# A hybrid decoder block on one core: the down projection of its MLP as seven products of halves

## The chip, the core and the metric

The kernel runs on one core of a Trainium2 chip. The core's engines work side by side, each through its own list of instructions in order: TensorE (PE, matrix products into PSUM), VectorE (DVE), ScalarE (ACT), GpSimd (POOL) and SyncE (SP), which issues the transfers from memory. They wait for each other by semaphores. The metric is the device time of one execution in microseconds (us).

## The reference

One layer on 512 tokens of width 1024, in float32: token mixing (attention heads and a short convolution), then the gated MLP. The part that matters here is its end.

```python
h = rms_norm(x, norm_ffn_pre[l])                        # (512, 1024)
gu = causal_dwconv(h @ w_ffn_up[l], ffn_conv_w[l])      # (512, 5632), a convolution of three taps
g, up = jnp.split(gu, 2, axis=-1)
y = (jax.nn.gelu(g, approximate=True) * up) @ w_ffn_down[l]   # (512, 2816) @ (2816, 1024)
x = x + rms_norm(y, norm_ffn_post[l])
```

## The kernel before

A float32 product runs as three passes over operands that are split exactly into a high and a low part: high x high, low x high, high x low. A split is two operations, one of ACT that rounds (`split`, L131, or `Stream._split`, L84) and one of DVE that subtracts (L132, L85). So each product of a 128x128 and a 128x512 tile is three matmuls.

The dense weights come through `Stream`: tiles of 128x1024 in the order of their use, loaded by SP into three raw buffers, split into a ring of four buffers, two tiles ahead of PE. Before the down projection, the up projection (L829 to L844) makes 44 tiles of 128 channels x 512 tokens. Per tile PE runs 24 matmuls from the transposed activations h2T (L166 to L169), ACT and DVE do the convolution (L825 to L827), and for each of the 22 pairs of gate and value ACT applies the gelu (L842), DVE multiplies (L843), and the product is split into aT (L844).

The down projection (L846 to L877) sums over the 22 tiles f of 128 channels. Each tile of weights (128 channels x 1024 columns) meets the activations of four token tiles t and two column halves hf: 8 x 3 = 24 matmuls a tile (`one`, L739), into all eight banks of PSUM, one for each (t, hf). After 19 tiles, the last three are taken token tile by token tile (`token_major`, L730), so that a finished one can be normed and stored while PE works on the next: ACT squares and sums (L865), DVE multiplies by the gains (L866), POOL takes the reciprocal root (`rstd_of`, L248), DVE multiplies and adds the residual (L873), SP stores. POOL has no other work in this stage.

The order on each engine is set by a scheduler when the program is built, mostly that of the code, with later instructions moved ahead where buffers are free.

Of the kernel before, what the change touches and what calls it, by code (L numbers as in the profile page):

```python
# [54 lines left out]
class Stream:  # L55
    """The dense weights in the order of their use: loaded some tiles ahead, split fewer ahead."""

    def __init__(self, tc, nc, raw, ring, items, loads=3, splits=2):
# [49 lines left out]
def block_kernel(ctx: ExitStack, tc: tile.TileContext, a, out):  # L108
# [52 lines left out]
    items += [(a["w_d"][f * P:(f + 1) * P, :], 1024, f"d{f}") for f in range(NF)]  # L161
# [31 lines left out]
    # the tensor engine's clock comes up while the first loads are under way  # L193
# [6 lines left out]
    # bias tables: U[p, h, u] = -(bias of distance p + 384 - u), +BIG where it is negative  # L200
    # row r of vrows is the whole of vd; reading with a pitch one short shifts it by r
# [544 lines left out]
    with tc.tile_pool(name="ph2", bufs=1, reuse_waits="tile") as ph2:  # L746
# [49 lines left out]
        # the first tiles of the MLP in halves of the tokens, behind the norm of the last rows  # L796
# [20 lines left out]
    ph3 = ctx.enter_context(tc.tile_pool(name="ph3", bufs=1, reuse_waits="tile"))  # L817
    aT = ph3.tile([P, NF, 2, S], F32R, name="aT")
# [12 lines left out]
    for n, m in enumerate(UP):  # L831
# [7 lines left out]
        if m >= NF:  # L839
# [13 lines left out]
    for f in range(NF - LAST):
        w = W.next()
        for th in banks:
            one(ys[th], dacts, w, f, *th, f == 0, False)
# [81 lines left out]
```

## Time and profile before

| what | us |
|---|---|
| median of the runs (634.5, 637.78, 637.83) | 637.78 |
| span of the profiled execution | 633.9 |
| up projection, PE | 272.0 to 507.6 |
| down projection, PE | 507.6 to 627.1 |
| its end, after the last matmul's start | 627.1 to 633.9 |

The profile is of one execution, whose own time is not given beside its span; by the runs it lies 0.6 to 3.9 us above it. A duration of a matmul overlaps its neighbours', so PE's pace is read from starts. In "idle before" the time stands that an engine waited, and what ended it.

### The profile page before, as it was taken

The page shows a single profiled execution, that of the slowest core. Times are in us where ns is not written, and L with a number is a line of the kernel's source. Part 1 is how long each engine was busy: PE and PEld are TensorE (multiplying, and loading weights), DVE is VectorE, ACT ScalarE, POOL GpSimd, SP SyncE. Part 2 cuts the span into 40 slices and gives each one's busy share as a digit, 9 for nine tenths or more (in the row PEclk, how much of TensorE's full clock was granted, in tenths as well). Part 3 has the DMA queues.
Part 4 walks back from the last instruction along what each step waited for, and adds up shares of the span by engine and source line. Part 5 has one row for each costly group of instructions (what it writes and reads, how often), then busy time and mean ns, then how long its engine had stood idle before and what let it go on. Part 6 is the DMA issues. An engine that isn't in the chain of part 4 may idle for free.

```text
span 633.9 us, 8027 instructions
## 1 busy us (share of the span) xinstructions
PE 617.5 (97%) x2980; PEld 511.3 (81%) x2980; DVE 382.2 (60%) x668; ACT 306.5 (48%) x556; POOL 62.7 (10%) x88
## 2 busy tenths in 40 slices
PE   8998899999999999999999999999999999999995
PEld 6886688887778788898888888888888888888884
DVE  5379967898988756648666656565656542222225
ACT  6546765798878644426443434444344422222212
POOL 1102453002130202200000000000000000000001
PEclk9999899999999999999999999999999999999999
DMA  8993355201121483004222233232322232232203
GB/s 293 329 304 129 133 180 189 74 10 43 42 78 53 169 280 130 8 5 143 93 96 98 99 100 101 100 100 99 101 87 95 89 114 87 94 100 99 67 0 133
DMA packets 25302, 72.00 MB, mean 114 GB/s; under 512 B 3136, under 2 KB 7048, under 8 KB 25008
## 3 DMA queue, kind: packets, MB, share of 16 engines
q1 hardware_dynamic: 25264, 71.50, 33.9%
q8 instruction: 23, 0.38, 0.2%
q14 instruction: 15, 0.12, 0.1%
HBM read 67.50 MB, written 4.74 MB: 114 GB/s over the span
## 4 chain that ended last, share of the span: by engine, by line
PE 80%; DVE 10%; DMA 3%; ACT 3%; issue 2%; POOL 1%; SPq 0%; DVEq 0%; POOLq 0%; ACTq 0%
PE pu L168 13%; PE pu L169 13%; PE pu L167 13%; PE z L743 6%; PE z L742 6%; PE z L744 6%; PE y L744 2%; PE y L743 2%; PE y L742 2%; DVE x L417 2%; DMA raw_q<-in_w_t 2%; PE tr L622 2%; PE sc L593 2%; PE o L631 1%; PE o L630 1%
## 5 line engine op out<-in xcount | busy, mean ns | idle before, releaser
L167 PE MATMUL pu<-h2T,w_u 128*128 128x512 f32 (+1 forms) x384 | 142.8, 372 | 0.0
L168 PE MATMUL pu<-h2T,w_u 128*128 128x512 f32 (+1 forms) x384 | 142.7, 372 | 0.0
L169 PE MATMUL pu<-h2T,w_u 128*128 128x512 f32 (+1 forms) x384 | 142.6, 371 | 0.0
L167 PEld LDWEIGHTS pu<-h2T,w_u 128*128 128x128 f32 x384 | 72.3, 188 | 12.6
L168 PEld LDWEIGHTS pu<-h2T,w_u 128*128 128x128 f32 x384 | 72.3, 188 | 12.6 <-DVE h2T L132 0.2
L169 PEld LDWEIGHTS pu<-h2T,w_u 128*128 128x128 f32 x384 | 72.3, 188 | 12.4
L826 DVE SCALAR_TENSOR_TENSOR cv<-pu,ffnw,cv 128x511 f32<-128x511 f32 x44 | 32.9, 749 | 70.2 <-ACT cv L825 70.2
L85 DVE TENSOR_TENSOR w_d<-raw_d,w_d 128x1024 fp32r<-128x1024 f32 x22 | 26.9, 1224 | 72.8 <-ACT w_d L84 72.8
L742 PE MATMUL z<-w_d,aT 128*128 128x512 f32 x176 | 68.5, 389 | 0.0
L743 PE MATMUL z<-w_d,aT 128*128 128x512 f32 x176 | 68.5, 389 | 0.0
L744 PE MATMUL z<-w_d,aT 128*128 128x512 f32 x176 | 68.5, 389 | 0.0
L825 ACT ACTIVATE cv<-pu,ffnw 128x512 f32<-128x512 f32 x44 | 30.3, 688 | 64.0 <-PE pu L169 63.9
L84 ACT ACTIVATE w_d<-raw_d 128x1024 fp32r<-128x1024 f32 x22 | 23.3, 1059 | 75.2 <-PE z L744 75.2
L85 DVE TENSOR_TENSOR w_u<-raw_u,w_u 128x1024 fp32r<-128x1024 f32 x44 | 53.4, 1217 | 5.9 <-ACT w_u L84 5.8
L84 ACT ACTIVATE w_u<-raw_u 128x1024 fp32r<-128x1024 f32 x44 | 46.2, 1052 | 6.6 <-PE pu L169 6.3
L599 ACT ACTIVATE P<-P,mins 128x512 f32<-128x512 f32 (+3 forms) x64 | 35.4, 554 | 11.5 <-DVE mins L597 11.1
L742 PEld LDWEIGHTS z<-w_d,aT 128*128 128x128 f32 x176 | 33.0, 188 | 6.9
L744 PEld LDWEIGHTS z<-w_d,aT 128*128 128x128 f32 x176 | 33.0, 188 | 6.9
L743 PEld LDWEIGHTS z<-w_d,aT 128*128 128x128 f32 x176 | 33.0, 188 | 6.7
L131 ACT ACTIVATE aT<-cv 128x512 fp32r<-128x512 f32 x22 | 13.9, 632 | 49.5 <-DVE cv L843 49.5
L251 POOL TENSOR_SCALAR rsz<-ssz 128x1 f32<-128x1 f32 x4 | 1.2, 300 | 355.2 <-ACT jz L865 355.2
L827 DVE SCALAR_TENSOR_TENSOR cv<-pu,ffnw,cv 128x510 f32<-128x510 f32 x44 | 32.8, 748 | 1.5
(215 smaller groups left out, 1158.7 us busy)
## 6 DMA issues: line engine op xcount, KB each, us to landing
raw_u<-in_w_u SPq DMA_DIRECT2D x44, 512.0 KB, 3.3
raw_d<-in_w_d SPq DMA_DIRECT2D x22, 512.0 KB, 3.2
raw_c<-in_w_c SPq DMA_DIRECT2D x8, 512.0 KB, 3.3
raw_o<-in_w_o SPq DMA_DIRECT2D x8, 512.0 KB, 3.4
vrows<-vd SPq DMA_DIRECT2D x2, 1280.0 KB, 10.4
xT<-in_xT SPq DMA_DIRECT2D x8, 256.0 KB, 5.3
xt<-in_x SPq DMA_DIRECT2D x4, 512.0 KB, 7.1
raw_q<-in_w_t SPq DMA_DIRECT2D x4, 512.0 KB, 7.0
```

Of the source, the lines that this page charges most:

```text
L84: self.nc.scalar.activation(t[:, 0, cs], self.raws[n][:, cs], AF.Copy)
L85: eng.tensor_tensor(t[:, 1, cs], self.raws[n][:, cs], f32(t[:, 0, cs]), op=ALU.subtract)
L167: MM(dst, wh, xh, start=first, stop=False)
L168: MM(dst, wh, xl, start=False, stop=False)
L169: MM(dst, wl, xh, start=False, stop=last)
L599: act(v, v, AF.Exp, bias=m, scale=-1.0, accum_out=self.sums[:, r, b:b + 1])
L742: MM(y, oh_, w[:, 0, cs], start=first, stop=False)
L743: MM(y, ol_, w[:, 0, cs], start=False, stop=False)
L744: MM(y, oh_, w[:, 1, cs], start=False, stop=last)
L825: act(t, pu, AF.Copy, scale=ffnw[:, m, 2:3])
L826: nc.vector.scalar_tensor_tensor(t[:, 1:], pu[:, :S - 1], ffnw[:, m, 1:2], t[:, 1:], op0=ALU.mult, op1=ALU.add)
L827: nc.vector.scalar_tensor_tensor(t[:, 2:], pu[:, :S - 2], ffnw[:, m, 0:1], t[:, 2:], op0=ALU.mult, op1=ALU.add)
```

## The change

The down product is cut in halves in three ways: tokens (0 to 255 and 256 to 511), channels (even and odd tiles f) and columns (0 to 511 and 512 to 1023). With A11, A12, A21, A22 the four parts of the activations (rows are tokens, columns are even and odd channels) and B11, B12, B21, B22 those of the weights, seven products take the place of eight:

- phase a: A11 x B11 into banks zx, (A21 + A22) x T1 into zy, with T1 = B12 - B11
- phase b: (A11 - A21) x (B22 - B12) into zw, S2 x T2 on top of zx, with S2 = A21 + A22 - A11 and T2 = B22 - T1
- phase c: A12 x B21 into zz, A22 x (B21 - T2) on top of zw
- phase d: (A12 - S2) x B22 on top of zy

Each phase runs over the 11 pairs j of channel tiles, d in six steps of two pairs and one. A product is 2 token tiles x 3 matmuls a pair, so a tile of a, b or c has 12 matmuls and each is still 128x128 by 128x512. The sums and differences of the weights are POOL's (L859, L865, L866, L872, L923), in the raw tile and in a tile `tres` that takes the buffer of h2T; those of the activations are POOL's too (L907, L911, L912 in the up stage, L939 later). What they give is split as before, now in pieces of 128x512 (`part`, L103, L104, and `split`, L149, L150). Between the phases the banks are copied (L985, L988, L1014) or added up (L1011, L1015); the two second products of b and c add onto banks that were filled before, and so begin after these reads. In phase d and behind it, what remains is added (L998) ahead of the square and the gains. The weights of the down projection are loaded by halves, those of B12, B21 and B22 apart; B22 and B12 twice.

```diff
+        if isinstance(src, list):
+            for at, part in src:
+                self.nc.sync.dma_start(t[:, at:at + 512], part)
...
+    def part(self, t, cs, src):
+        self.nc.scalar.activation(t[:, 0, cs], src, AF.Copy)
+        self.nc.vector.tensor_tensor(t[:, 1, cs], src, f32(t[:, 0, cs]), op=ALU.subtract)
...
-    items += [(a["w_d"][f * P:(f + 1) * P, :], 1024, f"d{f}") for f in range(NF)]
+    wd = lambda f, n: a["w_d"][f * P:(f + 1) * P, n * 512:(n + 1) * 512]
+    items += [(a["w_d"][2 * j * P:(2 * j + 1) * P, :], 1024, f"da{j}") for j in range(NJ)]
+    items += [([(0, wd(2 * j + 1, 1)), (512, wd(2 * j, 1))], 1024, f"db{j}") for j in range(NJ)]
+    items += [([(0, wd(2 * j + 1, 0))], 1024, f"dc{j}") for j in range(NJ)]
+    items += [([(512 * n, wd(2 * j + 1, 1)) for n, j in enumerate(js)], 512 * len(js), f"dd{js[0]}") for js in DJ]
...
+    def made_b(j):
+        def f(raw, t):
+            nc.gpsimd.tensor_tensor(raw[:, hi_], raw[:, lo_], raw[:, hi_], op=ALU.subtract)
+            nc.gpsimd.tensor_tensor(tres[j], raw[:, lo_], tres[j], op=ALU.subtract)
+            return (lo_, raw[:, hi_]), (hi_, tres[j])
+        return f
...
-            nc.vector.tensor_tensor(tg, tg, tu, op=ALU.mult)
-            split(aT[:, f, 0, :], aT[:, f, 1, :], tg)
+            if f % 2 == 0:
+                nc.vector.tensor_tensor(tg, tg, tu, op=ALU.mult)
+                even = tg.rearrange("p (m c) -> p m c", m=2)
+                nc.gpsimd.tensor_tensor(sb[:, jj, 0], even[:, 0], even[:, 1], op=ALU.subtract)
+            else:
+                odd = sc_[:, jj]
+                nc.vector.tensor_tensor(odd.rearrange("p m c -> p (m c)"), tg, tu, op=ALU.mult)
+                nc.gpsimd.tensor_tensor(even[:, 1], even[:, 1], odd[:, 1], op=ALU.add)
+                nc.gpsimd.tensor_tensor(sb[:, jj, 1], even[:, 1], even[:, 0], op=ALU.subtract)
+                t = ah["a", jj] = acts_tile(f"aa{jj}")
+                split(t[:, 0], t[:, 1], even)
...
+    whole = hpool.tile([P, 16, 512], F32, tag="hT", name="tres")
...
+            split(t[:, 0], t[:, 1], src[:, j])
+            if ph == "b":
+                nc.gpsimd.tensor_tensor(sb[:, j, 1], sc_[:, j, 0], sb[:, j, 1], op=ALU.subtract)
...
+    phase("a", (bx, by), (True, True), 2)
+    c1, c57, c2 = [], [], []
+    for m in range(2):
+        c1.append(spare[m])
+        act(c1[m], bx[m], AF.Copy)
...
+    phase("b", (bw, bx), (True, False), 1)
...
+    for m in range(2):
+        nc.vector.tensor_tensor(c57[m], bw[m], c57[m], op=ALU.add)
...
+    phase("c", (bz, bw), (True, False), 1)
...
+    for m in range(2):
+        for n in range(tail, len(DJ)):
+            for i in range(len(DJ[n])):
+                prod(by, m, tiles[n], ah["d", n], i, False, n == len(DJ) - 1 and i == len(DJ[n]) - 1)
+        half_done(m, 1, by[m], c2[m])
+        tile_done(m)
```

Where the emitted order differs. On POOL, before, the norm of the last rows of the mixing part (rs) is followed at once by the first of the MLP's four (rsz):

```order
L252 TENSOR_TENSOR rsy3_2754<-rsy3_2754,mhalf_122 128x1
L251 TENSOR_SCALAR rs2_3_2762<-ss2_3_2757 128x1
L252 TENSOR_TENSOR rs2_3_2762<-rs2_3_2762,mhalf_122 128x1
L251 TENSOR_SCALAR rsz0_5067<-ssz0_5049 128x1
L252 TENSOR_TENSOR rsz0_5067<-rsz0_5067,mhalf_122 128x1
```

On POOL, after, this stands at the edge of phases a and b (raw_da and raw_db are loaded weights, tres the differences, sb and sc activations, of 256 tokens each half):

```order
L859 TENSOR_TENSOR tres_4499<-raw_da10_4626 128x512
L866 TENSOR_TENSOR tres_4499<-raw_db0_4646,tres_4499 128x512
L865 TENSOR_TENSOR raw_db0_4646<-raw_db0_4646 128x512
L939 TENSOR_TENSOR sb_3010<-sc_3011,sb_3010 128x256
L866 TENSOR_TENSOR tres_4499<-raw_db1_4667,tres_4499 128x512
L865 TENSOR_TENSOR raw_db1_4667<-raw_db1_4667 128x512
L939 TENSOR_TENSOR sb_3010<-sc_3011,sb_3010 128x256
```

Between rs2_3 and the first rsz there were no rows, and there are now 88 operations: 33 of 128x256 on the activations of the up stage, and 44 of 128x512 on the weights with 11 of 128x256 among them, the first four of these ahead of the up stage's last two.

On DVE, before, the down stage has one split a tile of weights and nothing else:

```order
L85 TENSOR_TENSOR w_d15_4865<-raw_d15_4781,w_d15_4865 128x1024
L85 TENSOR_TENSOR w_d16_4894<-raw_d16_4810,w_d16_4894 128x1024
L85 TENSOR_TENSOR w_d17_4923<-raw_d17_4839,w_d17_4923 128x1024
L85 TENSOR_TENSOR w_d18_4952<-raw_d18_4868,w_d18_4952 128x1024
L85 TENSOR_TENSOR w_d19_4981<-raw_d19_4897,w_d19_4981 128x1024
```

On DVE, after, at the edge of b and c (w_db and w_dc are split weights, ac the split activations of phase c, zw a bank of PSUM):

```order
L104 TENSOR_TENSOR w_db10_4961<-raw_db10_4892,w_db10_4961 128x512
L104 TENSOR_TENSOR w_db10_4961<-tres_4499,w_db10_4961 128x512
L150 TENSOR_TENSOR ac6_5176<-sc_3011,ac6_5176 128x512
L104 TENSOR_TENSOR w_dc0_4986<-raw_dc0_4918,w_dc0_4986 128x512
L104 TENSOR_TENSOR w_dc0_4986<-tres_4499,w_dc0_4986 128x512
L150 TENSOR_TENSOR ac7_5200<-sc_3011,ac7_5200 128x512
L104 TENSOR_TENSOR w_dc1_5010<-raw_dc1_4943,w_dc1_5010 128x512
L104 TENSOR_TENSOR w_dc1_5010<-tres_4499,w_dc1_5010 128x512
L150 TENSOR_TENSOR ac8_5224<-sc_3011,ac8_5224 128x512
L104 TENSOR_TENSOR w_dc2_5041<-raw_dc2_4968,w_dc2_5041 128x512
L104 TENSOR_TENSOR w_dc2_5041<-tres_4499,w_dc2_5041 128x512
L1011 TENSOR_TENSOR tres_4499<-zw0_4510,tres_4499 128x512
```

A tile now takes three operations of half the size in place of one, and the read of zw stands nine operations behind the last split of phase b.

On DVE, before, the last two token halves end the program like this (z a bank, tz its normed rows):

```order
L866 TENSOR_TENSOR tz30_5153<-z30_4486,gpo_5035 128x512
L866 TENSOR_TENSOR tz31_5166<-z31_4487,gpo_5035 128x512
L873 SCALAR_TENSOR_TENSOR tz30_5153<-tz30_5153,rsz3_5169,x1_2408 128x512
L873 SCALAR_TENSOR_TENSOR tz31_5166<-tz31_5166,rsz3_5169,x1_2408 128x512
```

On DVE, after, the last rows are of token tiles 0 and 1 (zy a bank, c2 a copy of another):

```order
L998 TENSOR_TENSOR tz01_5425<-zy0_4508,c20_5035 128x512
L1000 TENSOR_TENSOR tz10_5390<-tz10_5390,gpo_4514 128x512
L1000 TENSOR_TENSOR tz01_5425<-tz01_5425,gpo_4514 128x512
L1007 SCALAR_TENSOR_TENSOR tz00_5384<-tz00_5384,rsz0_5430,x1_2408 128x512
L1007 SCALAR_TENSOR_TENSOR tz01_5425<-tz01_5425,rsz0_5430,x1_2408 128x512
L998 TENSOR_TENSOR tz11_5446<-zy1_4509,c21_5038 128x512
L1000 TENSOR_TENSOR tz11_5446<-tz11_5446,gpo_4514 128x512
L1007 SCALAR_TENSOR_TENSOR tz10_5390<-tz10_5390,rsz1_5451,x1_2408 128x512
L1007 SCALAR_TENSOR_TENSOR tz11_5446<-tz11_5446,rsz1_5451,x1_2408 128x512
```

An addition has come ahead of ACT's square, and the last one stands behind both products of the tile before.

## Rows read from the trace of the kernel before

**Rows 1.** The page's head and its busy times by engine.
```profile
span 633.9 us, 8027 instructions
...
PE 617.5 (97%) x2980; PEld 511.3 (81%) x2980; DVE 382.2 (60%) x668; ACT 306.5 (48%) x556; POOL 62.7 (10%) x88
```

**Rows 2.** Two stretches, up and down projection; columns in the first line.
```profile
core 0: us, PE busy (x) PEld busy (x) DVE busy (x) ACT busy (x) POOL busy (x), PEclk, DMA share, GB/s
272.00:507.60 235.60, 235.60 (x1113) 198.19 (x1112) 142.51 (x175) 100.35 (x134) 0.00 (x0) 1.00 0.29 95
507.60:627.10 119.50, 119.50 (x529) 98.91 (x527) 34.63 (x36) 26.18 (x35) 2.58 (x6) 1.00 0.24 83
```

**Rows 3.** In order of time, PE (start us, duration us, instruction).
```profile
507.63 0.39 PE L742 MATMUL z<-w_d,aT 128*128 128x512 f32 x1
...
508.31 0.39 PE L742 MATMUL z<-w_d,aT 128*128 128x512 f32 x1
```

**Rows 4.** Groups by line, down stage (xcount, busy us, mean ns, idle before).
```profile
L742 PE MATMUL z<-w_d,aT 128*128 128x512 f32 x176 | 68.5, 389 | 0.0
...
L85 DVE TENSOR_TENSOR w_d<-raw_d,w_d 128x1024 fp32r<-128x1024 f32 x19 | 23.3, 1225 | 72.8 <-ACT w_d L84 72.8
```

**Rows 5.** In order of time, POOL, then DVE, near 182 us.
```profile
182.59 1.09 POOL L505 TENSOR_TENSOR cz<-cz,Rb 128x512 f32<-128x512 f32 x1 [2.60 <-DVE sums L604]
...
182.62 1.09 DVE L606 TENSOR_TENSOR sums<-sums,G 128x2 f32<-128x2 f32 x1
```

**Rows 6.** In order of time, POOL, then DVE, 100 to 107 us.
```profile
100.30 1.09 POOL L505 TENSOR_TENSOR cz<-cz,Rb 128x512 f32<-128x512 f32 x1 [4.63 <-DVE cz L504]
...
105.16 2.19 POOL L511 TENSOR_TENSOR ct<-ct,Rb 128x512 f32<-128x512 f32 x1 [2.12 <-DVE ct L509]
...
100.62 1.85 DVE L85 TENSOR_TENSOR w_tx<-raw_tx,w_tx 128x1024 fp32r<-128x1024 f32 x1 [0.40 <-ACT w_tx L84]
...
105.00 1.21 DVE L85 TENSOR_TENSOR w_tb<-raw_tb,w_tb 128x1024 fp32r<-128x1024 f32 x1
```

**Rows 7.** In order of time, POOL, then DVE, near 187 us.
```profile
187.47 1.29 POOL L511 TENSOR_TENSOR ct<-ct,Rb 128x512 f32<-128x512 f32 x1 [2.07 <-DVE ct L509]
...
187.64 0.69 DVE L132 TENSOR_TENSOR ptl<-tr,pth 128x512 fp32r<-128x512 f32 x1
```

**Rows 8.** In order of time, POOL near 81 us.
```profile
81.10 2.41 POOL L85 TENSOR_TENSOR w_c<-raw_c,w_c 128x1024 fp32r<-128x1024 f32 x1 [2.60 <-ACT w_c L84]
```

**Rows 9.** In order of time, DVE, two operations back to back.
```profile
72.71 0.68 DVE L132 TENSOR_TENSOR ptl<-tr,pth 128x512 fp32r<-128x512 f32 x1
73.31 0.68 DVE L372 TENSOR_TENSOR qt<-pp_q,Rb 128x512 f32<-128x512 f32 x1
```

**Rows 10.** The page's DMA issues, loads of the down weights.
```profile
raw_d<-in_w_d SPq DMA_DIRECT2D x22, 512.0 KB, 3.2
```

**Rows 11.** In order of time, all engines, the kernel's end.
```profile
627.08 0.39 PE L744 MATMUL z<-w_d,aT 128*128 128x512 f32 x1
627.57 0.60 ACT L865 ACTIVATE jz<-z 128x512 f32<-128x512 f32 x1 [1.33 <-PE z L744]
...
628.35 0.30 POOL L251 TENSOR_SCALAR rsz<-ssz 128x1 f32<-128x1 f32 x1 [3.14 <-ACT jz L865]
628.73 0.56 POOL L252 TENSOR_TENSOR rsz<-rsz,mhalf 128x1 f32<-128x1 f32 x1
629.33 1.41 DVE L873 SCALAR_TENSOR_TENSOR tz<-tz,rsz,x 128x512 f32<-128x512 f32 x2 [0.35 <-POOL rsz L252]
```

**Rows 12.** In order of time, PE; then a stretch (columns: rows 2).
```profile
64.25 0.40 PE L167 MATMUL pp_q<-hT,w_q 128*128 128x512 f32 x1
67.60 0.45 PE L622 MATMUL tr<-ident,P 128*128 128x128 f32 x1 [2.96 <-ACT P L613]
67.71 0.77 PE L168 MATMUL pp_q<-hT,w_q 128*128 128x512 f32 x1
...
68.00:70.00 2.00, 2.00 (x7) 1.51 (x6) 1.92 (x4) 1.84 (x4) 0.00 (x0) 0.50 0.04 14
```

More of the change, by code (lines that the diff above doesn't have):

```diff
@@ L39 @@
 NF = DFF // P
+NJ = NF // 2
+DJ = [list(range(j, min(j + 2, NJ))) for j in range(0, NJ, 2)]
 EPS = 1e-6
@@ L66, in __init__ @@
         self.other = {}
+        self.made = {}
+        self.cap = 10000
     def _load(self):
@@ L79, in _split @@
         t = pool.tile([P, 2, 1024], F32R, tag=tag, bufs=bufs, name=f"w_{name}")
+        if name in self.made:
+            for cs, src in self.made[name](self.raws[n], t):
+                self.part(t, cs, src)
+            self.tiles.append(t)
+            return
         eng = self.nc.gpsimd if name in self.pool_lo else self.nc.vector
@@ L817, in block_kernel, with acts_tile, made_a, f @@
     ph3 = ctx.enter_context(tc.tile_pool(name="ph3", bufs=1, reuse_waits="tile"))
-    aT = ph3.tile([P, NF, 2, S], F32R, name="aT")
+    sb = ph3.tile([P, NJ, 2, 256], F32, name="sb")
+    sc_ = ph3.tile([P, NJ, 2, 256], F32, name="sc")
+    def acts_tile(name):
+        return ph3.tile([P, 2, 2, 256], F32R, tag="ah", bufs=NJ, name=name)
+    ah = {}
+    lo_, hi_ = slice(0, 512), slice(512, 1024)
+    tres, late_t1 = [], []
+    def made_a(j):
+        def f(raw, t):
+            if not tres:
+                late_t1.append((j, raw, t))
+                return [(lo_, raw[:, lo_])]
+            nc.gpsimd.tensor_tensor(tres[j], raw[:, hi_], raw[:, lo_], op=ALU.subtract)
+            return (lo_, raw[:, lo_]), (hi_, tres[j])
+        return f
+    def made_b(j):
+        def f(raw, t):
+            nc.gpsimd.tensor_tensor(raw[:, hi_], raw[:, lo_], raw[:, hi_], op=ALU.subtract)
+            nc.gpsimd.tensor_tensor(tres[j], raw[:, lo_], tres[j], op=ALU.subtract)
+            return (lo_, raw[:, hi_]), (hi_, tres[j])
+        return f
+    def made_c(j):
+        def f(raw, t):
+            nc.gpsimd.tensor_tensor(tres[j], raw[:, lo_], tres[j], op=ALU.subtract)
+            return (lo_, raw[:, lo_]), (hi_, tres[j])
+        return f
+    for j in range(NJ):
+        W.made[f"da{j}"], W.made[f"db{j}"], W.made[f"dc{j}"] = made_a(j), made_b(j), made_c(j)
+    W.cap = next(n for n, x in enumerate(W.items) if x[2] == "da0") + 3
     def cv(name):
@@ L853, in block_kernel @@
[L853 to L856, printed above, removed]
+            jj = f // 2
+            if f % 2 == 0:
+                nc.vector.tensor_tensor(tg, tg, tu, op=ALU.mult)
+                even = tg.rearrange("p (m c) -> p m c", m=2)
+                nc.gpsimd.tensor_tensor(sb[:, jj, 0], even[:, 0], even[:, 1], op=ALU.subtract)
+            else:
+                odd = sc_[:, jj]
[4 more added lines that the diff above has]
+                split(t[:, 0], t[:, 1], even)
@@ new lines, in block_kernel, with acts_ready @@
+    W.cap = 10000
+    whole = hpool.tile([P, 16, 512], F32, tag="hT", name="tres")
+    tres += [whole[:, j] for j in range(NJ)]
+    spare = [whole[:, 12 + n] for n in range(4)]
+    for j, raw, t in late_t1:
+        nc.gpsimd.tensor_tensor(tres[j], raw[:, hi_], raw[:, lo_], op=ALU.subtract)
+        W.part(t, hi_, tres[j])
+    def acts_ready(ph, j):
+        if ph == "a" or (ph, j) in ah:
+            return
+        t = ah[ph, j] = acts_tile(f"a{ph}{j}")
+        if ph == "d":
+            js = DJ[j]
+            n = slice(0, len(js))
+            split(t[:, 0, n], t[:, 1, n], sb[:, js[0]:js[-1] + 1, 1])
+        else:
+            src = sb if ph == "b" else sc_
+            split(t[:, 0], t[:, 1], src[:, j])
+            if ph == "b":
+                nc.gpsimd.tensor_tensor(sb[:, j, 1], sc_[:, j, 0], sb[:, j, 1], op=ALU.subtract)
@@ new lines, in block_kernel, with prod @@
+    bx = [pt_bank(f"zx{m}") for m in range(2)]
+    by = [sc_bank(f"zy{m}") for m in range(2)]
+    bw = [mm_bank(f"zw{m}") for m in range(2)]
+    bz = [mm_bank("zz0"), o_bank("zz1")]
+    def prod(bk, m, t, x, n, first, last):
+        cs = slice(n * 512, (n + 1) * 512)
+        tok = slice(m * P, (m + 1) * P)
+        MM(bk[m], x[:, 0, n, tok], t[:, 0, cs], start=first, stop=False, skip_group_check=True)
+        MM(bk[m], x[:, 1, n, tok], t[:, 0, cs], start=False, stop=False, skip_group_check=True)
+        MM(bk[m], x[:, 0, n, tok], t[:, 1, cs], start=False, stop=last, skip_group_check=True)
@@ new lines, in phase, with second @@
+    def phase(ph, banks, opens, skew):
+        tiles = []
+        def second(j):
+            for m in range(2):
+                prod(banks[1], m, tiles[j], ah[ph, j], 1, opens[1] and j == 0, j == NJ - 1)
+        for j in range(NJ):
+            w = W.next()
+            acts_ready(ph, j)
+            tiles.append(w)
+            for m in range(2):
+                prod(banks[0], m, w, ah[ph, j], 0, opens[0] and j == 0, j == NJ - 1)
+            if j == skew:
+                for i in range(skew):
+                    second(i)
+            if j >= skew:
+                second(j)
+            nxt = {"a": "b", "b": "c", "c": "d"}[ph]
+            if j + 1 < NJ:
+                acts_ready(ph, j + 1)
+            elif ph != "c":
+                acts_ready(nxt, 0)
@@ L857, in block_kernel, with half_done @@
     gpo = ph3.tile([P, D], F32, name="gpo")
     nc.sync.dma_start(gpo, a["g_ffn_post"].broadcast_to([P, D]))
+    phase("a", (bx, by), (True, True), 2)
[3 more added lines that the diff above has]
+        act(c1[m], bx[m], AF.Copy)
+    for m in range(2):
+        c57.append(spare[2 + m])
+        act(c57[m], by[m], AF.Copy)
+    phase("b", (bw, bx), (True, False), 1)
     fin = {}
-    def half_done(t, hf):
-        if hf == 0:
+    def half_done(t, hf, y, other):
+        if t not in fin:
@@ L874, in tile_done @@
             nc.sync.dma_start(out[t * P:(t + 1) * P, cs], fin[t, hf])
-    wl = [W.next(1) for _ in range(LAST)]
-    token_major(wl, ys, dacts, half_done, tile_done, list(range(NF - LAST, NF)))
+    for m in range(2):
+        nc.vector.tensor_tensor(c57[m], bw[m], c57[m], op=ALU.add)
+    for m in range(2):
+        c2.append(cv(f"c2{m}"))
+        act(c2[m], bx[m], AF.Copy)
+        nc.vector.tensor_tensor(c57[m], bx[m], c57[m], op=ALU.add)
+    phase("c", (bz, bw), (True, False), 1)
+    tail = len(DJ) - 2
+    tiles = []
+    for n, js in enumerate(DJ):
+        w = W.next(2)
+        tiles.append(w)
+        acts_ready("d", n)
+        if n + 1 < len(DJ):
+            acts_ready("d", n + 1)
+        if n < tail:
+            for m in range(2):
+                for i in range(len(js)):
+                    prod(by, m, w, ah["d", n], i, False, False)
+        if n == 0:
+            for m in range(2):
+                t = 2 + m
+                fin[t] = stat(f"ssz{t}")
+                half_done(t, 0, bw[m], c2[m])
+        if n == 1:
+            for m in range(2):
+                t = 2 + m
+                tt, junk = cv(f"tz{t}1"), cv(f"jz{t}1")
+                act(junk, c57[m], AF.Square, scale=1.0 / 32.0, accum_out=fin[t][:, 1:2])
+                nc.vector.tensor_tensor(tt, c57[m], gpo[:, 512:], op=ALU.mult)
+                fin[t, 1] = tt
+                tile_done(t)
+        if n == 2:
+            for m in range(2):
+                half_done(m, 0, bz[m], c1[m])
+    for m in range(2):
+        for n in range(tail, len(DJ)):
[3 more added lines that the diff above has]
+        tile_done(m)
 def _bucket_onehot():
```

18 lines of the change are left out of this document (7 added, 11 removed).

## The prediction

> **What bounds the kernel now.** I read the page's head and the table of stretches first. TensorE (PE) is busy for 97% of the 633.9 us, VectorE (DVE) for 60%, GpSimd (POOL) for 10% [rows 1]. In the down projection, 507.6 to 627.1, PE is busy for all of 119.50 us at the full clock, DVE for 34.63 and POOL for 2.58 [rows 2]: the stage is bound by its matmuls alone. Its pace is read from starts, since the durations overlap: one operand triple begins at 507.63 and the next at 508.31 [rows 3], so a matmul costs 0.68 / 3 = 0.2267 us, and 528 of them 119.7 us, which is the stage. One DVE split of 1.22 us per 24 matmuls (5.44 us) lies under them [rows 4]. The span ends 6.6 us after the last matmul's slot (627.08 + 0.23).
>
> Against its own time: the profiled execution's span is 633.9 us; the runs shown are 634.5 to 637.83 with median 637.78, so 0.6 to 3.9 us lie around a span. I work out the change of the span and add it to the median.
>
> **What goes.** Seven products of halves need 7/8 of the matmuls: 66 fewer of 528, 66 x 0.2267 = **-15.0 us**. The 33 tiles of phases a, b and c have 12 matmuls each, 2.72 us a tile and 29.9 us a phase; phase d has 66, 15.0 us.
>
> **What comes: a shared resource.** Each tile now has combinations on POOL and twice the splits on DVE: per tile of a one POOL subtraction of 128x512, of b two (the weights) and mostly one of 128x256, of c one; on DVE two splits of weights and one of activations, 128x512 each. Taken alone each engine fits, or nearly: 2 x 1.29 + 0.72 = 3.3 us of POOL and 3 x 0.60 of DVE in b. The question is whether they run at the same time. The rows say no. At 182.59 POOL reads two tiles for 1.09 us, and a DVE operation on 128x2, begun 0.03 us later, lasts 1.09 us too [rows 5]. At 100.30 POOL works until 101.39; DVE's split, begun at 100.62, lasts 1.85 us instead of 1.22 and ends 1.08 us after POOL. At 105.00 DVE begins first and ends at 106.21; POOL, begun at 105.16, lasts 2.19 and ends 1.14 us after DVE [rows 6]. While one of them runs, the other stands, and then needs most of its own time. A DVE operation with one operand in PSUM (tr) ran in its ordinary 0.69 us beside POOL [rows 7], so only DVE operations with two SBUF operands count: all the splits of the down stage.
>
> [...]
>
> Prices in the queue: POOL 128x512 alone 1.29 [rows 7], after a DVE operation 1.14 [rows 6]. 128x1024 takes 2.41 [rows 8], so 512 elements more cost 1.13; 128x256 is then about 0.72 alone (estimate), 0.58 in the queue. DVE 128x512 in the queue: half of 1.08, 0.54, say 0.55; back to back 0.60 (72.71 to 73.31) [rows 9].
>
> **The walk.** PE begins phase a at 507.6 as before. The tile for the differences takes h2T's place, so POOL cannot begin before the last up matmul: three subtractions from 507.9. The load of da3 needs the raw buffer of da0, free after the second of them (507.9 + 2 x 1.29 = 510.5), and lands 3.2 us later [rows 10], at 513.7. From there the queue is full. Until the last POOL operation of phase b, the two orders hold 30 POOL operations of 512, 13 of 256 and 54 DVE splits: 30 x 1.14 + 13 x 0.58 + 54 x 0.55 = 34.2 + 7.5 + 29.7 = 71.4 us, to 585.1. PE, unhindered, would have finished b at 507.6 + 59.8 = 567.4. This is the main cost: **about 18 us late at that point**.
>
> Then the edge of b and c. The second product of c adds onto the banks zw, which DVE must first read (L1011), and in DVE's order that read stands behind the splits of dc0 to dc2. From 585.1: three POOL subtractions, each with a DVE split (1.69), then POOL waits for a load and eight DVE splits run at 0.60: 5.1 + 4.8 = 9.9, to 595.0; the read 0.7, so PE goes on at 595.7. By then it has done 12 of c's 132 matmuls; 120 x 0.2267 = 27.2 brings it to 622.9. POOL and DVE have less than that left in c (8 x 1.14, 23.5 x 0.55 and four reads at 0.60: 24.5), so PE bounds c from there. Phase d has no POOL work, its 1.22 us splits lie under 2.72 us of matmuls: 15.0, to 637.9.
>
> The like edge of a and b (the copy L985 stands on ScalarE behind the splits of db2) leaves PE idle for about 5 us at 549 to 554, but b waits for the queue anyway, and PE's 2.72 us a tile against the queue's 4.0 to 4.5 makes it up. Cost 0; without that cover about 5.
>
> The end. Before, from the last slot (627.31): ScalarE at 627.57, POOL's root, DVE's two last products to 630.74 (629.33 + 1.41), then 3.2 to the span's end [rows 11]. After, the last half is first added to c2 on DVE (0.73), and that add (tz11) stands behind tile 0's two products. Tile 0's last matmul lies 9 x 0.2267 = 2.04 before the end; its add (0.26 + 0.73) and the 3.17 us from ScalarE's start to the products' end make 4.16, so tz11 begins 2.12 after the last slot, and its own chain ends 2.12 + 0.73 + 3.17 = 6.02 after it, against 3.43 before: **+2.6 us**.
>
> Sum: 637.9 + 6.6 + 2.6 = 647.1 against 633.9: **+13.2 us**. On the median: **651 us**.
>
> Edits priced at nothing. In the up stage, three POOL operations of 256 per four up tiles (21.8 us): DVE there is busy for 142.51 of 235.60 us [rows 2], which hides 2.2 us of blocking per 21.8; uncovered it would be 11 x 2.2 = 24 us, which I exclude since PE there is fed two splits ahead. The loads grow from 11 to 17 MB; the DMA engines are busy for 24% [rows 2]. The matmuls' shape is the same.
>
> Bounds of the queue: with POOL at the quickest two-input row (1.09, 0.95 in the queue) 30 x 0.19 = 5.7 us less; with every operation at its full price alone (1.29, 0.72, DVE 0.60), 80.5 instead of 71.4, 9.1 us more. I take the middle value because rows 6 show this very alternation. Span +7.5 to +22.
>
> **Rivals.**
> 1. *They run side by side after all* (the stalls of rows 5 and 6 were waits for something else). Then b is bound by POOL at 22 x 1.29 + 6 x 0.72 = 32.7 against 29.9, and the change is -15.0 + 2.8 + 2.6 + 1 at the start = -8.6: 629 us. Against it: an operation on two columns stretched to POOL's 1.09 us.
> 2. *The queue is shorter, and comes out even.* POOL at 0.95 and 0.46, and the edge at L1011 gone since POOL's last three subtractions are already done when DVE comes to ac6 (-5): 71.4 - 5.7 - 1.6 - 5 gives about +1: 639 us. For it: the 1.09 of rows 5 and 6; against it: the 1.09 reads from column 2 on (L505), the operations here from aligned columns, as L511 with its 1.29 [rows 7].
> [...]
> 4. *It computes something else, or not seven products*: the emitted order of PE has 66 matmuls fewer, so no.
>
> **How the numbers follow.** Slower by the queue, 642 to 660: 0.73. Rival 3: 0.10. Rival 2: 0.09. Rival 1: 0.08. About 0.5% (3.2 us) is what a measurement of this kernel tells from no change, so "same" is 634.6 to 641. Faster 0.08; same 0.10 (rival 2 and the low edge of the forecast); slower 0.82. The range for 8 in 10 is 640 to 661: it leaves out rival 1, most of rivals 2 and 3.
>
> **What would show it.** PE in the down stage: 462 matmuls and about 20 us idle, most of it in phase b, where PE waits for DVE's splits. DVE's 128x512 splits there have a mean well over 0.69 us (near 1.2 to 1.7), POOL's subtractions over 1.29 (near 1.7). A row of POOL and a row of DVE overlap in time, but the later one ends about one own duration after the earlier. The last slot lies near 638, and 9 us follow it. Wrong it would be if DVE's splits keep 0.69 beside a working POOL (rival 1), if PE's idle time in b is under 5 us (rival 2), or if the granted clock is near 0.5 through b (rival 3).

## The result, and the profile after

The changed kernel takes 655.97 us (median of 4 runs, 654.34 to 656.36) where the one before takes 636.14 (633.9 to 637.83): a ratio of 1.0322, with a 95% interval of 1.0286 to 1.0358. The forecast was 651, counted on the median of 637.78 known then (a ratio of 1.021), with a range of 640 to 661, slower. The span of the profiled execution is 652.6 us, 18.7 more than before; the forecast was +13.2.

The table of stretches of the kernel after, one row for each of the phases a, b, c and d (columns as in [rows 2]):

```profile
506.40:542.30 35.90, 32.16 (x133) 24.08 (x132) 34.27 (x30) 17.77 (x31) 30.19 (x22) 1.00 0.47 159
542.30:589.40 47.10, 36.80 (x133) 25.39 (x132) 47.10 (x35) 22.17 (x42) 41.81 (x28) 0.93 0.33 108
589.40:627.40 38.00, 32.99 (x133) 26.40 (x132) 34.08 (x40) 18.66 (x31) 14.05 (x9) 0.91 0.39 124
627.40:642.40 15.00, 15.00 (x67) 12.21 (x65) 12.64 (x19) 7.27 (x17) 4.57 (x5) 1.00 0.26 91
```

Before, one row answered to these four: 119.50 us with PE busy in all of it [rows 2]. Now a, b and c take 35.9, 47.1 and 38.0 where 12 x 11 matmuls need 29.9 each, and only d, without weight differences, runs at PE's pace. In b the busy engines are DVE (all 47.10) and POOL (41.81), and yet their 35 and 28 operations would take some 24 and 32 us at the durations of undisturbed ones (0.68 on DVE, as at 585.34; on POOL 1.29 to 1.30 for 128x512, as in [rows 7] and at 506.64, and 0.74 for 128x256, as at 303.9). The groups of b show the same by their means (128x512 each; xcount | busy us, mean ns):

```profile
L865 POOL TENSOR_TENSOR raw_db<-raw_db 128x512 f32<-128x512 f32 x11 | 19.0, 1728 | 0.0
L866 POOL TENSOR_TENSOR tres<-raw_db,tres 128x512 f32<-128x512 f32 x11 | 18.5, 1684 | 2.2 <-DMA raw_db<-in_w_d 2.2
L104 DVE TENSOR_TENSOR w_db<-tres,w_db 128x512 fp32r<-128x512 f32 x11 | 18.4, 1671 | 0.0
...
L104 DVE TENSOR_TENSOR w_db<-raw_db,w_db 128x512 fp32r<-128x512 f32 x11 | 17.2, 1565 | 0.0
```

How that comes about is seen in single rows of b, POOL first, then DVE, in order of time (start, duration):

```profile
557.03 1.74 POOL L865 TENSOR_TENSOR raw_db<-raw_db 128x512 f32<-128x512 f32 x1
558.73 1.19 POOL L939 TENSOR_TENSOR sb<-sc,sb 128x256 f32<-128x256 f32 x1
559.88 1.74 POOL L866 TENSOR_TENSOR tres<-raw_db,tres 128x512 f32<-128x512 f32 x1
561.59 1.73 POOL L865 TENSOR_TENSOR raw_db<-raw_db 128x512 f32<-128x512 f32 x1
```

```profile
557.54 1.77 DVE L104 TENSOR_TENSOR w_db<-tres,w_db 128x512 fp32r<-128x512 f32 x1
559.24 1.23 DVE L150 TENSOR_TENSOR ab<-sb,ab 128x512 fp32r<-128x512 f32 x1
560.39 1.78 DVE L104 TENSOR_TENSOR w_db<-raw_db,w_db 128x512 fp32r<-128x512 f32 x1
562.09 1.77 DVE L104 TENSOR_TENSOR w_db<-tres,w_db 128x512 fp32r<-128x512 f32 x1
```

Read the ends: POOL's row of 557.03 ends at 558.77, DVE's of 557.54 at 559.31, 0.54 later; POOL's next ends at 559.92, 0.61 after that. Both engines are "busy" without a gap, but at each moment one of them works and the other's row is running while it waits. The period of a pair is 559.24 - 557.54 = 1.70 us, for 1.14 + 0.55 = 1.69 forecast; with a 128x256 it is 1.15, for 1.13.

The edge of b and c, PE's row with its wait and DVE's read:

```profile
592.49 0.51 PE L952 MATMUL zz<-w_dc,ac 128*128 128x512 f32 x1 [1.05 <-DVE w_dc L104]
597.65 0.79 PE L950 MATMUL zw<-w_dc,ac 128*128 128x512 f32 x1 [3.96 <-DVE tres L1011]
598.25 0.63 PE L951 MATMUL zw<-w_dc,ac 128*128 128x512 f32 x1
598.67 0.63 PE L952 MATMUL zw<-w_dc,ac 128*128 128x512 f32 x1
...
602.92 0.40 PE L950 MATMUL zz<-w_dc,ac 128*128 128x512 f32 x1
```

```profile
595.25 1.75 DVE L104 TENSOR_TENSOR w_dc<-tres,w_dc 128x512 fp32r<-128x512 f32 x1
596.92 1.28 DVE L1011 TENSOR_TENSOR tres<-zw,tres 128x512 f32<-128x512 f32 x2
```

PE stands for 4 us until the read is done. The twelve matmuls behind it start 0.60, then 0.41 to 0.43 us apart in place of 0.2267, and the granted clock in 598.0 to 602.6 is 0.50.

The end, rows of PE, DVE, ACT, POOL in order of time (they answer to [rows 11]):

```profile
642.14 0.39 PE L952 MATMUL zy<-w_dd,ad 128*128 128x512 f32 x1
...
643.61 1.41 DVE L1007 SCALAR_TENSOR_TENSOR tz<-tz,rsz,x 128x512 f32<-128x512 f32 x2 [0.84 <-POOL rsz L277]
...
644.94 0.68 DVE L998 TENSOR_TENSOR tz<-zy,c 128x512 f32<-128x512 f32 x1
645.71 0.63 ACT L999 ACTIVATE jz<-tz 128x512 f32<-128x512 f32 x1 [3.68 <-DVE tz L998]
...
646.47 0.69 DVE L1000 TENSOR_TENSOR tz<-tz,gpo 128x512 f32<-128x512 f32 x1 [0.85 <-ACT jz L999]
646.53 0.79 POOL L276 TENSOR_SCALAR rsz<-ssz 128x1 f32<-128x1 f32 x1 [2.96 <-ACT jz L999]
647.41 0.56 POOL L277 TENSOR_TENSOR rsz<-rsz,mhalf 128x1 f32<-128x1 f32 x1
648.00 1.41 DVE L1007 SCALAR_TENSOR_TENSOR tz<-tz,rsz,x 128x512 f32<-128x512 f32 x2 [0.84 <-POOL rsz L277]
```

From the last matmul's start to the span's end it is now 652.6 - 642.14 = 10.5 us; before, 633.9 - 627.08 = 6.8.

### The profile page after: what moved, and what is told of

The parts are those of the page before. It is cut to its first block, busy times and chain, and to the rows that moved or that the text cites. A ratio compares the mean times of both kernels' runs of the same rounds, so it can differ in the third digit from the quotient of the medians.

```text
span 652.6 us, 8230 instructions
## 1 busy us (share of the span) xinstructions
PE 613.5 (94%) x2914; PEld 499.3 (77%) x2914; DVE 467.8 (72%) x745; ACT 336.9 (52%) x629; POOL 176.4 (27%) x176
## 4 chain that ended last, share of the span: by engine, by line
PE 69%; DVE 22%; issue 3%; ACT 3%; POOL 2%; DMA 1%; SPq 0%; DVEq 0%; POOLq 0%; ACTq 0%
PE pu L193 12%; PE pu L192 12%; PE pu L194 12%; DVE w_db L104 5%; PE y L768 2%; PE y L769 2%; PE y L767 2%; DVE w_da L104 2%; DVE x L442 2%; PE tr L647 2%; PE sc L618 2%; DVE ab L150 2%; DVE ac L150 2%; PE o L656 1%; PE zw L950 1%
## 5 line engine op out<-in xcount | busy, mean ns | idle before, releaser
L907 POOL TENSOR_TENSOR sb<-cv 128x256 f32<-128x256 f32 x11 | 9.1, 826 | 110.1 <-DVE cv L905 110.1
L636 POOL TENSOR_SCALAR P<-P,sums 128x512 f32<-128x512 f32 (+3 forms) x16 | 9.6, 603 | 97.9 <-DVE sums L631 66.8
L911 POOL TENSOR_TENSOR cv<-cv,sc 128x256 f32<-128x256 f32 x11 | 8.4, 763 | 96.8 <-DVE sc L910 92.0
L622 DVE CUSTOM_DVE_ANT_0 P<-sc,U 128x512 f32<-128x512 f32 (+3 forms) x64 | 30.3, 483 | 3.0 <-PE sc L618 1.9
L647 PE MATMUL tr<-ident,P 128*128 128x128 f32 x160 | 26.8, 276 | 4.7 <-ACT P L638 3.0
L618 PE MATMUL sc<-KK,Q 128*128 128x256 f32 (+2 forms) x112 | 30.1, 350 | 1.1 <-DVE mins L622 0.5
L150 DVE TENSOR_TENSOR ptl<-tr,pth 128x512 fp32r<-128x512 f32 x40 | 27.3, 684 | 2.9 <-ACT pth L149 2.5
L647 PEld LDWEIGHTS tr<-ident,P 128*128 128x128 f32 x160 | 20.1, 142 | 11.4 <-ACT P L638 4.1
L638 ACT ACTIVATE P<-P,sums 128x512 f32<-128x512 f32 (+3 forms) x48 | 24.6, 554 | 6.6 <-DVE sums L631 6.4
L149 ACT ACTIVATE pth<-tr 128x512 fp32r<-128x512 f32 x40 | 23.6, 590 | 3.3 <-PE tr L647 3.0
```

Of the source, the lines that this page charges most:

```text
L618: MM(sc[:, :n], q, k, start=s == 0, stop=s == 1)
L647: nc.tensor.transpose(tr[:, r * P:(r + 1) * P], self.p[r][:, c0:c0 + P], ident)
```

## The experiments

Each is the changed kernel with one edit more, but for the last four, which build on each other. A theory of turns (POOL and DVE exclude each other) stood against the rivals that POOL's subtractions are slow by themselves, and that DVE's work is too much by itself.

**No differences of weights.** POOL's 44 subtractions go; the operands are the raw halves.

```diff
-            nc.gpsimd.tensor_tensor(raw[:, hi_], raw[:, lo_], raw[:, hi_], op=ALU.subtract)
-            nc.gpsimd.tensor_tensor(tres[j], raw[:, lo_], tres[j], op=ALU.subtract)
-            return (lo_, raw[:, hi_]), (hi_, tres[j])
+            return (lo_, raw[:, hi_]), (hi_, raw[:, lo_])
...
```

and so for the subtractions of phases a and c.

> The 44 subtractions of weights (POOL, 128x512) are left out; T1, T2 and the other differences are replaced by the raw halves, so seven products of other operands are computed, with the same matmuls, splits and loads. Theory 1 (POOL and DVE take turns): DVE's 128x512 splits in phase b fall from 1.57 to 1.67 us to about 0.68 (0.60 from start to start), a and b are bound by PE, 29.9 us each, and the edge of b and c loses its gap: the stage is 462 x 0.2267 = 104.7 us and perhaps 2 more, against 136.0 measured, so the span is 652.6 - 29 = about 623. Theory 2 (POOL's subtractions are slow by themselves, and DVE only waits for them): the same gain. Theory 3 (the 33 more splits on DVE and ACT are too many by themselves): phase b stays over 40 us, the span over 640.

One run: 622.99 us, span 621.2. Its stretches a to d:

```profile
506.30:536.20 29.90, 29.90 (x133) 24.76 (x132) 26.28 (x35) 19.63 (x36) 11.01 (x11) 1.00 0.55 183
536.20:566.10 29.90, 29.90 (x133) 24.77 (x132) 21.76 (x35) 19.76 (x37) 1.48 (x2) 1.00 0.47 153
566.10:596.00 29.90, 29.90 (x133) 24.77 (x132) 20.41 (x32) 16.36 (x28) 0.00 (x0) 1.00 0.43 140
596.00:611.00 15.00, 15.00 (x67) 12.21 (x66) 12.64 (x19) 7.27 (x17) 4.53 (x5) 1.00 0.25 91
```

PE has no gap: 104.7 us, the 462 matmuls at 0.2267. So the 15.0 us that the seven products save are real, the 31 us that phases a to c take beyond PE's own all go with the subtractions, and so does the gap at the edge: the read of zw is in time when the queue is not there. The theory that DVE and ACT have too much to do by themselves is out.

**No low parts of the weights.** The subtractions stay, DVE's splits go.

```diff
     def part(self, t, cs, src):
         self.nc.scalar.activation(t[:, 0, cs], src, AF.Copy)
-        self.nc.vector.tensor_tensor(t[:, 1, cs], src, f32(t[:, 0, cs]), op=ALU.subtract)
...
-        MM(bk[m], x[:, 0, n, tok], t[:, 1, cs], start=False, stop=last, skip_group_check=True)
+        MM(bk[m], x[:, 0, n, tok], t[:, 0, cs], start=False, stop=last, skip_group_check=True)
```

> DVE's 66 subtractions that give the low parts of the weights of phases a, b and c are left out, and the third matmul of each triple reads the high part in their place; POOL's subtractions all stay. Theory 1 (turns): POOL's 128x512 falls from 1.73 us to 1.3, except beside the one split of activations a tile; phase b is 11 x (2 x 1.25 + 0.6 + 0.55) = 40 us at most, in place of 47.1, phase a near 30 in place of 36, and the edge of b and c is short: span about 632 to 638. Theory 2 (POOL slow by itself): POOL's operations stay at 1.73, b stays at 45 or more.

One run: 628.24 us, span 626.4, below the 632 to 638 expected. POOL's subtractions in phase b, by line:

```profile
L864 POOL TENSOR_TENSOR raw_db<-raw_db 128x512 f32<-128x512 f32 x10 | 15.1, 1512 | 0.0
L865 POOL TENSOR_TENSOR tres<-raw_db,tres 128x512 f32<-128x512 f32 x9 | 13.0, 1441 | 0.0
```

In the changed kernel the two groups have 1728 and 1684 ns, and 1290 undisturbed. POOL is not slow by itself: with a third of DVE's splits left beside it, its operations lose about half of their stretch or more. The size was missed because I let all of b's POOL work fall into b: only 19 of its 22 subtractions and 5 of its 11 smaller ones lie there, the others in a; b took 33.4 us, not 40.

**One operand in PSUM.** ScalarE copies the difference into a free bank, and DVE subtracts from that.

```diff
     def part(self, t, cs, src, bank=None):
         self.nc.scalar.activation(t[:, 0, cs], src, AF.Copy)
+        if bank is not None:
+            self.nc.scalar.activation(bank, src, AF.Copy)
+            src = bank
```

> In phase b ScalarE also copies B22 - B12 into a free bank of PSUM, and DVE's low part of it subtracts from that copy: the same operation with one operand in PSUM and one in SBUF; everything else as in the changed kernel, one copy of 0.6 us a tile more on ScalarE. Theory 1, two SBUF operands are what excludes POOL: w_db<-bank splits take 0.7 us beside a working POOL instead of 1.57, the tile of b goes from 4.5 to 3.95 us, 11 x 0.55 = 6 us: ratio to before 1.022 in place of 1.032. Theory 1b, any DVE operation excludes POOL: the splits stay near 1.6 and the time at 1.032, or a little more for ScalarE's copies.

648.98 us, ratio 1.0227 (1.0182 to 1.0272). The group of DVE, then two rows of POOL and DVE that overlap:

```profile
L107 DVE TENSOR_TENSOR w_db<-pb,w_db 128x512 fp32r<-128x512 f32 x11 | 7.5, 686 | 4.5 <-ACT w_db L103 4.3
```

```profile
562.50 0.74 POOL L943 TENSOR_TENSOR sb<-sc,sb 128x256 f32<-128x256 f32 x1 [0.73 <-DVE ab L153]
```

```profile
562.34 0.68 DVE L107 TENSOR_TENSOR w_db<-pb,w_db 128x512 fp32r<-128x512 f32 x1
562.94 0.85 DVE L107 TENSOR_TENSOR w_db<-tres,w_db 128x512 fp32r<-128x512 f32 x1
```

The split from the bank pb runs at its own 0.68 beside a POOL row that keeps its own 0.74; the next split, with two operands in SBUF, begins at 562.94 and is held until POOL ends at 563.24. The group's mean goes from 1565 to 686 ns. The splits from the bank at 549.72, 553.36 and 575.90 keep 0.69 beside 128x512 rows of POOL that keep 1.27 to 1.29. Shown by these rows: what excludes POOL is two SBUF operands, not a DVE operation as such. The total came out as forecast only in part by this mechanism: b went from 47.1 to 40.0 us and c from 38.0 to 35.5, but a from 35.9 to 40.2, where PE stood 3.8 us at 536.8 in a new order.

**The differences on DVE.**

```diff
-            nc.gpsimd.tensor_tensor(raw[:, hi_], raw[:, lo_], raw[:, hi_], op=ALU.subtract)
+            nc.vector.tensor_tensor(raw[:, hi_], raw[:, lo_], raw[:, hi_], op=ALU.subtract)
```

and so for the other four lines.

> The 44 subtractions of weights go from POOL to DVE; only the activations' (128x256) stay on POOL. Theory 1 (turns, and each turn of POOL costs 1.14 us): each costs 0.60 of DVE's own time instead, so the work up to the end of b is 30 x 0.60 + 13 x 0.58 + 54 x 0.60 = 57.9 us instead of 71.4, no longer over PE's 59.8; the nine splits ahead of the read of zw are done sooner. Span 652.6 - 14 to 18 = 635 to 639, ratio 1.00 to 1.01. If the two engines did work side by side (no turns), taking the subtractions from POOL to DVE would only load DVE: 44 x 0.6 = 26 us more on the busier engine, and the time would rise or stay.

637.04 us, ratio 1.0032 (1.0007 to 1.0056), span 636.1: by the two ratios some 18 us less than with the work shared between two engines. Phases a and b:

```profile
506.50:541.20 34.70, 32.61 (x133) 25.61 (x132) 31.14 (x48) 21.66 (x39) 5.92 (x5) 0.95 0.56 183
541.20:579.60 38.40, 32.90 (x133) 26.62 (x133) 34.98 (x53) 19.93 (x37) 9.11 (x8) 0.91 0.41 129
```

DVE has 18 operations more in a and 18 more in b and is busy for less time. If the two engines had worked side by side, this edit would have cost time.

**The edge alone.** The splits of dc1 and dc2 are put behind the read of zw.

```diff
+    W.after = read.ins
...
-            with self.tc.high_priority(30) if self.early else nullcontext():
+            with self.tc.issue_after(self.after) if self.after else self.tc.high_priority(30) if self.early else nullcontext():
                 self._split()
```

> The changed kernel with another order at the edge of phases b and c alone: DVE reads zw (the sum with c57) after dc0's splits, and the splits of dc1 and dc2 are issued behind that read. Theory A (the 4.12 us gap of PE at 593.3 to 597.65 and the half clock behind it come from the place of that read): zw is done at about 588, the read ends near 589.5, the splits of dc1 near 592, and PE goes on at 592.4 in place of 597.65; 5 us and about 2 us of half clock are gone, of which the queue of POOL and DVE takes 0 to 2 back in c. Span 646 to 648, ratio about 1.022. Theory B (c would be bound by the queue anyway): the gap is spread over c's tiles and the ratio stays at 1.030 or more.

653.76 us, ratio 1.0301 (1.0274 to 1.0328), span 650.5: 2.1 us less than the changed kernel's span, where theory A said 4.6 to 6.6. The interval of the ratio overlaps that of the changed kernel, so no gain is shown. PE now waits for the split that was put back:

```profile
594.32 0.80 PE L952 MATMUL zz<-w_dc,ac 128*128 128x512 f32 x1 [2.89 <-DVE w_dc L104]
```

Theory A has fallen, and B has the better of it: behind the read's place there stands the queue, and whichever of its products PE needs first comes late. The half clock came here too (granted clock 0.50 in 594 to 600; the rows at 594.32 and 594.91 last 0.80 and 0.63 us).

**The end alone.**

```diff
         half_done(m, 1, by[m], c2[m])
+    for m in range(2):
         tile_done(m)
```

> The changed kernel with another order at its end alone: the last half of token tile 1 is added (tz11) before tile 0 is multiplied by its root. The add then starts about 0.5 us after the last matmul in place of 2.7, and the tail from the last matmul's start to the span's end falls from 10.4 to about 8.2 us: ratio 1.029 in place of 1.032. If the tail hangs on the two tiles' stores or on ScalarE, it stays at 10.4.

652.98 us, ratio 1.0297 (1.0269 to 1.0325), span 650.6. The intervals of the ratios overlap, so the gain is read from the trace: the tail is 8.5 us in place of 10.5. The add, the two steps of POOL's root and the last products:

```profile
642.67 0.68 DVE L998 TENSOR_TENSOR tz<-zy,c 128x512 f32<-128x512 f32 x1
...
644.27 0.83 POOL L276 TENSOR_SCALAR rsz<-ssz 128x1 f32<-128x1 f32 x1 [0.71 <-ACT jz L999]
...
645.18 0.85 POOL L277 TENSOR_TENSOR rsz<-rsz,mhalf 128x1 f32<-128x1 f32 x1
646.07 1.42 DVE L1007 SCALAR_TENSOR_TENSOR tz<-tz,rsz,x 128x512 f32<-128x512 f32 x2 [0.45 <-POOL rsz L277]
```

The place of tz11's add cost 2.0 us. The other 1.6 are the add itself, ahead of ACT's square (642.67 to 643.45, 0.8), and POOL's root, whose two steps take 0.83 and 0.85 us beside DVE's products with two SBUF operands, in place of 0.30 and 0.56 [rows 11] (another 0.8).

**Towards a faster kernel.** First: differences on DVE, A12 - S2 made in the up stage, the end's new order.

```diff
-            if ph == "b":
-                nc.gpsimd.tensor_tensor(sb[:, j, 1], sc_[:, j, 0], sb[:, j, 1], op=ALU.subtract)
...
+                nc.gpsimd.tensor_tensor(sd[:, jj], odd[:, 0], sb[:, jj, 1], op=ALU.subtract)
```

> All subtractions of weights on DVE, as in e4_diff_dve; A12 - S2 is made in the up stage by POOL into a buffer of its own (eleven operations of 128x256 fewer in the down stage; ten buffers of split activations in place of eleven), and the end in the order of e6_tail. POOL has no work in the down stage but the roots. DVE's own work in a to c is 44 x 0.60 + 66 x 0.60 + 28 x 0.60 + 4 x 0.7 = 86 us, under PE's 89.8. Theory (turns): no DVE row is stretched, e4's 636.1 falls by 2.2 for the end and by some 5 of the 13 us that a and b still lost: span 626 to 631, ratio 0.985 to 0.995, faster than before. If DVE's own work is what bounds a and b, the gain over e4 is the end's 2.2 alone: ratio 1.000.

636.13 us, ratio 1.0010 (0.9987 to 1.0033): no measurable change, against 0.985 to 0.995 expected. Its runs lie far apart (632.35 to 638.04), and the profiled one, a span of 630.6, is among the shortest; what the longer ones lost stands in no trace. In b of the profiled run PE stood once for 3.6 us:

```profile
557.67 0.73 PE L952 MATMUL zw<-w_db,ab 128*128 128x512 f32 x1 [3.64 <-DVE ab L150]
```

Second, the splits of activations are written three pairs ahead of PE's need, and in each pair ahead of the next weights:

```diff
+            acts_ready(ph, j)
             w = W.next()
-            acts_ready(ph, j)
...
-            if j + 1 < NJ:
-                acts_ready(ph, j + 1)
+            for i in (j + 1, j + 2, j + 3):
+                if i < NJ:
+                    acts_ready(ph, i)
+                elif ph != "c":
+                    acts_ready(nxt, i - NJ)
```

> e10_sd with the splits of activations written up to three pairs ahead instead of one. In e4_diff_dve PE stood for 5.7 us at 557.6 to 563.4 and went on when DVE's split of ab was done, which stood behind four weight operations. If that order is what is left, another 2 to 5 us go: span 623 to 628, ratio 0.98 to 0.99. If the sum of DVE's work is the bound, it is as e10_sd within 1 us.

629.72 us, ratio 0.9928 (0.9903 to 0.9953): 0.7% less than before, where 0.98 to 0.99 was expected. The wait in b is gone (29.9 us, PE's own); a has 35.3.

Third, the first two T1 go first in DVE's order:

```diff
+    with tc.high_priority(400):
         for j, raw, t in late_t1:
```

> e12_sdacts with the T1 of the first two pairs (L925) put first in DVE's order at the start of the down stage, before the up stage's last convolution. In e12 PE lost 5.1 us in phase a: gaps of 0.4, 0.9 and 1.9 us at 515 to 520.4 and the half clock behind them, the last ended by ScalarE's copy of da1's T1, which DVE made fifth. If that order is the cause, phase a goes from 35.3 to 30 to 31 us and the span from 629.8 to about 625: ratio 0.985. If DVE's sum of work is the bound, the gaps come back later in a and b, ratio 0.993 as e12.

627.18 us, ratio 0.9871 (0.9846 to 0.9896), span 625.4. Its phases a, b, c:

```profile
508.80:538.70 29.90, 29.90 (x133) 24.77 (x132) 28.69 (x45) 19.62 (x34) 3.29 (x3) 1.00 0.65 211
538.70:570.00 31.30, 31.30 (x134) 24.40 (x133) 30.99 (x52) 20.66 (x38) 0.00 (x0) 1.00 0.49 152
570.00:602.20 32.20, 30.76 (x133) 24.53 (x132) 32.12 (x52) 18.43 (x31) 0.00 (x0) 1.00 0.42 138
```

Phase a is at PE's pace; in b and c DVE has hardly a gap left (30.99 of 31.30, 32.12 of 32.20) and is the bound, by 1.4 and 2.3 us. Fourth, one more tile of cover before the read of zw:

```diff
-    phase("c", (bz, bw), (True, False), 1)
+    phase("c", (bz, bw), (True, False), 2)
```

> e13_t1 with PE's second product of phase c two tiles behind the first in place of one (18 matmuls of zz, 4.1 us, before the first on zw). In e12 PE stood 1.5 and 1.0 us at 576.4 to 579.9 for DVE's reads of zw, and ran at half the clock behind it: c took 32.6 us in place of 29.9. With the cover both go: 2.5 us less than e13, span about 622.5, ratio 0.981. If the reads are later still by DVE's queue, no more than 1 us.

626.71 us, ratio 0.9871 (0.9851 to 0.9891): the same. DVE is busy for 32.10 of the 32.70 us of c. With DVE full, cover for PE brings nothing, as the expectation's second case had it. The half clock that the expectation saw in e12 at 576.4 to 579.9 is not in its rows: behind the second stop PE's starts are 0.23 us apart (580.21 to 582.96).

## Why the prediction was right, step by step

- **Matmuls, -15.0 us: right.** 462 x 0.2267 = 104.7, and that is the stage without the subtractions.
- **POOL and DVE take turns: right,** by rows and by four edits. Rival 1 (side by side) would have made the fourth edit slower; it made it some 18 us faster. The sign of the whole change hung on two rows [rows 5, 6].
- **The queue's length: right within 2 us.** POOL's last subtraction for b was to end at 585.1 and ended at 583.2, with a start 1.2 us earlier. The start is not the change's: the up stage begins anywhere from 263.6 to 266.3 in the variants here. It took 242.5 us in both executions (265.13 to 507.63 before, 263.89 to 506.39 after), so the three POOL operations per four up tiles cost nothing, as priced.
- **The edge of b and c: mis-sized, 13.8 us for 9.9.** The walk had three POOL subtractions, each with a stretched split, and then eight splits at 0.60. Measured from 583.16 (the end of POOL's last subtraction for b) to 596.92: 0.5 left of a split, then five stretched ones and eight short ones (5 x 1.70 + 8 x 0.60 = 13.3). Two things differ from the walk. The loads that I let POOL wait for came in time for two more subtractions, dc3 and dc4, each of which stretches a split by 1.1 us:

```profile
592.38 1.79 POOL L872 TENSOR_TENSOR tres<-raw_dc,tres 128x512 f32<-128x512 f32 x1 [1.70 <-DMA raw_dc<-in_w_d]
595.19 1.26 POOL L872 TENSOR_TENSOR tres<-raw_dc,tres 128x512 f32<-128x512 f32 x1 [1.01 <-DMA raw_dc<-in_w_d]
```

And when POOL's last subtraction ended, DVE had 13 splits and the rest of one ahead of the read, where the walk had 11: 1.7 us that the walk had put before that point. PE went on at 597.65, not 595.7: +2.0 us, the edge's 3.9 less the 1.9 by which the queue was early. Of those 1.9, 1.2 are the earlier start, so from PE's first matmul of phase a the walk was short by 3.2 us, and the two turns that it left out are most of that.

- **The clock in c: not in the sum.** Measured, at a granted clock of 0.50, the twelve matmuls behind the read took 5.3 us (597.65 to 602.92) for 2.7, and c from there 29.8 for 27.2: +2.6. The fall at the edge of a and b (549 to 556, granted clock 0.57) was hidden by the queue, as that edge was.
- **Phase d, 15.0 us: right.**
- **The end: +2.6 forecast, +3.6 measured.** The term of tz11's place was nearly right in size (2.0 by the edit). The walk took POOL's root at its old price, and left out a turn there. Before, DVE's product with the gains read a bank of PSUM, and the root's first step beside it took 0.30 us [rows 11]:

```profile
628.28 0.69 DVE L866 TENSOR_TENSOR tz<-z,gpo 128x512 f32<-128x512 f32 x1 [1.02 <-ACT jz L865]
```

Now the product (L1000) reads two SBUF tiles, and that step takes 0.79 us at 642.13 and again at 646.53, 0.5 us more in the chain of each token tile.

Together 2.0 + 2.6 + 1.0 = 5.6 against the 5.5 us by which the span passed the forecast; without the chance of a start 1.2 us early it would have been near 6.7. Rival 2 (an even result by a shorter queue and no edge) and rival 3 (half clock all through b) did not come: in b's regular tiles the granted clock was 1.00 (556 to 589.4).

## What to carry to other kernels

Before work is moved to an idle GpSimd, look in the trace for a GpSimd row and a VectorE row with two SBUF operands that overlap: if the later one ends one own duration after the other (here 1.08 us after it for a split of 1.22 [rows 4, 6]), the idle engine has no time to give, and 44 subtractions that cost 0.60 us each on VectorE cost 1.14 of both. Busy shares don't show this, since a waiting row counts as busy (DVE for all 47.10 us of b); a mean duration above that of the same operation elsewhere does (1728 ns in b for POOL's 1290). And an algorithm that saves 1/8 of the matmuls gains only as far as the engine that prepares the operands has room: here 15 us on PE, of which the best order kept about 8.

## What the hardware showed that I had not expected

- The length of PE's stop alone did not decide the clock. In the changed kernel a stop of 2.1 us (546.27 to 548.64), with shorter ones around it, was followed by a granted clock of 0.57 in 549 to 556; in the kernel without low parts a stop of 2.9 us (539.02 to 542.12, after more than 30 us without one) left it at 1.00, in 542.1 to 546 and over the whole of b (536.5 to 569.9). In the changed kernel three stops of 1.3 to 1.9 us, one a tile of b from 565 to 577, left it at 1.00 too, with PE busy for 12.08 of the 17.00 us from 560. The row is of the kernel without low parts, the two stretches are of the changed kernel:

```profile
542.12 0.50 PE L949 MATMUL zx<-w_db,ab 128*128 128x512 f32 x1 [2.71 <-ACT tres L984]
```

```profile
549.00:556.00 7.00, 6.28 (x17) 4.47 (x17) 7.00 (x6) 4.87 (x10) 7.00 (x6) 0.57 0.47 147
560.00:577.00 17.00, 12.08 (x46) 7.74 (x46) 17.00 (x12) 7.17 (x13) 16.71 (x11) 1.00 0.30 104
```
